# An FNet and Hyena encoder layer: another start of the Fourier stage, and the first batch's gate products on VectorE

## The chip, the cores and the metric

The kernel runs on one core of a Trainium2 chip. The metric is the device time of one execution in microseconds (us). The core has TensorE (PE, with its weight loads as PEld), VectorE (DVE), ScalarE (ACT), GpSimd (POOL) and SyncE (SP), which only starts transfers here. SP, ACT and POOL each have a queue of transfers of their own.

## What is computed

There are two batches, the prompt (b = 0) and the sample (b = 1), of 1024 rows with 1024 channels, in fp32. Each goes through the same layer:

```python
xn = rmsnorm(x, g_pre)
fv, fg, hv, hg, mg = split(xn @ w_in)
# Fourier branch: 4 groups of 256 channels
fz = real(fft2(fv.reshape(B, L, 4, 256), over rows and channels of a group, ortho))
y_f = (fz * silu(fg)) @ w_fourier_out
# Hyena branch: width-3 convolution, then two long gated convolutions
v, x1, x2 = split(short_conv(hv, w_short))
z = v
for n, gate in enumerate((x1, x2)):
    z = gate * long_conv(z, filters[n], hyena_d[n])   # two-sided, by FFT
y_h = (z * silu(hg)) @ w_hyena_out
g_f, g_h = split(sigmoid(mg + b_merge))
out = (g_f * y_f + g_h * y_h) @ w_out
y = x + rmsnorm(out, g_post)
```

The filters come from a small network with sine activations (`hidden`, two layers) and exponential decays.

## The kernel before

All products are made of fp32 operands split into a rounded high part and a remainder: `split` rounds on ScalarE (L171 in before) and subtracts on VectorE or POOL (L181), and `mm3` makes three matmuls of the four parts. `mm` is L194, so nearly all matmuls have that line; they are told apart by their tile names. Engines run their instructions in order. The order is made when the program is built, by a scheduler with a timeline of its own. `issue_after(i)` is the means against it: whatever is traced inside the block stands behind instruction `i` on `i`'s engine. Tiles have a tag and a number of buffers; a tile waits until its buffer's last user has finished.

The stages, by time in the profile:

- The Fourier stage (0 to some 225 us, `phase_fourier`). `hidden(0)` makes the filter network's first layer. `norm` loads x in eight row tiles of 128, squares each with a sum (`ss`), makes the reciprocal roots in two groups of four (`rstd`, many tiny VectorE instructions) and scales the identity by them (`dg`). `xtile(b, k)` makes channel tile k of the normalized x, transposed: eight matmuls of a row tile with `dg` (`tpx`), a scaled copy (`xg`, two buffers), a store to DRAM (`d_x`), the even and odd folding about the middle row (`eo`), and its split (`eh`, `el`). Row 512 of the folding goes into `x5` by itself, in two tiny VectorE instructions for each tile. `weights` loads and folds the columns of the Fourier projection (`wfv`, `wer`, `wor`; split into `we`, `wo`), in two halves. The products `pfv` of `begun` are accumulated tile by tile as `xtile` goes on, for the first batch only; six PSUM tiles are open then, and the other two odd ones follow. `fourier_half` then applies the row transform (`stage`, table `seq`: tiles `pse`, `pso`, `sev`, `sst`, `pp`, `qp`) and the channel transform (`pP`, `pQ`), and stores `fz`. The halves run as (0,0), (0,1), (1,1), (1,0).
- The main stage (`phase_main`, to some 765 us). It rebuilds split x from `d_x` (`xl`, `xh`), makes the filters' spectra (`pft`, `pXf`) and spills input projections for later (`spill_gate`, `pin`). Its first tables of the filters (`hid`, `w3s`, `ex`) come at the end of the Fourier stage.
- The branches (to some 1740 us, `branches`). 32 steps of long convolutions, 16 for each batch: projection and short convolution (`conv`), forward transform (`pX`), product with the spectrum (`t`, `y`, `yl`), inverse (`pT`). In the second convolution of the first batch, the gate x2 is multiplied by silu(hg) in two halves of 128x512 (`close`), on POOL.
- The gates of the second batch (`pg`) and the output stage (`phase_out`; `pyf`, `pyh`, then `po`). In the latter `gated` loads a gate tile `g`, and `ahead` loads and splits the operands of the next projection.

## Time and profile before

| | |
|---|---|
| median of 3 runs | 2445.93 us (2445.39 to 2446.81) |
| the profiled execution | 2449.26 us |
| its span | 2447.1 us |
| TensorE busy | 2396.1 us (98%), 13196 matmuls |
| VectorE busy | 1893.8 us (77%) |
| ScalarE busy | 1096.8 us (45%) |
| POOL busy | 485.9 us (20%) |
| transfers | 429.36 MB, 175 GB/s on average |

Busy times are by engine over the span; the profile also gives them for any stretch of time. A matmul's end is modelled, so that a busy TensorE need not be at its peak; the number of matmuls in a stretch says more. In a row of the groups or the timeline `out<-in` are the tiles, and what stands in brackets or behind the bar is the idle time of the engine before the instruction and who ended it.

### The profile page before, as it was taken

What the parts mean: (1) busy time and instruction counts of PE and PEld (TensorE: products, weight loads), DVE (VectorE), ACT (ScalarE), POOL (GpSimd) and SP (SyncE); (2) the same over time, 40 slices, a digit from 0 to 9 for tenths busy, and PEclk for the clock granted to TensorE, in tenths of its full rate; (3) what the DMA queues carried; (4) which work ended last, traced back from release to release, by engine and by line L of the source; (5) the groups of instructions that cost most, each with busy time, mean ns of one, the idle gap of its engine ahead of it and who ended that gap; (6) DMA issues with size and microseconds to landing.
All of it is one profiled execution on the core that took longest, in us unless ns stands there. A gap on an engine that the chain in (4) does not pass through costs nothing.

```text
span 2447.1 us, 36853 instructions
## 1 busy us (share of the span) xinstructions
PE 2396.1 (98%) x13196; PEld 2082.3 (85%) x13196; DVE 1893.8 (77%) x3405; ACT 1096.8 (45%) x2063; POOL 485.9 (20%) x516
## 2 busy tenths in 40 slices
PE   6999999999999999999999999999999999999998
PEld 5988888888888888888888888888788888888886
DVE  7687888888748999999989999766555455665677
ACT  5545677767633433334223333333344444544343
POOL 1341222222143433331000000112200111122111
PEclk9999999999999999999999999999999999999999
DMA  7545655555555555445434444335454567776543
GB/s 273 170 141 191 224 175 173 167 175 167 173 194 177 172 177 173 165 165 192 146 128 134 141 141 138 121 121 184 154 174 159 198 210 255 245 250 213 169 164 129
DMA packets 225151, 429.36 MB, mean 175 GB/s; under 512 B 23542, under 2 KB 87255, under 8 KB 224456
## 3 DMA queue, kind: packets, MB, share of 16 engines
q1 hardware_dynamic: 198444, 333.34, 41.1%
q0 software_dynamic: 26336, 93.65, 10.9%
q8 instruction: 104, 1.70, 0.3%
q14 instruction: 79, 0.65, 0.1%
q10 hardware_dynamic: 188, 0.02, 0.0%
HBM read 290.60 MB, written 136.31 MB: 174 GB/s over the span
## 4 chain that ended last, share of the span: by engine, by line
PE 88%; DMA 5%; issue 3%; DVE 2%; ACT 1%; POOL 1%; SPq 0%; DVEq 0%; POOLq 0%; ACTq 0%
PE pin L194 41%; PE pT L194 7%; PE pg L194 7%; PE pX L194 7%; PE po L194 6%; PE pyh L194 5%; PE pyf L194 5%; PE pXf L194 3%; PE pfv L194 2%; DMA wr<-in_w_fo 1%; PE pft L194 1%; PE tph L792 1%; DMA wr<-in_w_ho 1%; PE tpx L194 1%; DMA wfv<-in_w_fv 1%
## 5 line engine op out<-in xcount | busy, mean ns | idle before, releaser
L194 PE MATMUL pin<-xh,wl 128*128 128x512 f32 x1472 | 577.2, 392 | 2.6 <-POOL wl L181 2.6
L194 PE MATMUL pin<-xl,wh 128*128 128x512 f32 x1472 | 575.6, 391 | 2.4 <-DVE xl L181 2.4
L194 PE MATMUL pin<-xh,wh 128*128 128x512 f32 x1472 | 576.5, 392 | 0.7 <-DMA wh<-d_w 0.7
L181 POOL TENSOR_TENSOR wl<-wr,wh 128x512 fp32r<-128x512 f32 x136 | 240.3, 1768 | 1144.0 <-ACT wh L171 1105.9
L194 PEld LDWEIGHTS pin<-xh,wl 128*128 128x128 f32 x1472 | 277.1, 188 | 54.9 <-POOL wl L181 4.1
L194 PEld LDWEIGHTS pin<-xl,wh 128*128 128x128 f32 x1472 | 277.1, 188 | 54.3 <-DVE xl L181 3.2
L194 PEld LDWEIGHTS pin<-xh,wh 128*128 128x128 f32 x1472 | 277.1, 188 | 52.1 <-DMA wh<-d_w 1.1
L171 ACT CAST wh<-wr 128x512 fp32r<-128x512 f32 x264 | 162.8, 619 | 346.0 <-PE pin L194 136.8
L194 PE MATMUL pT<-cinv,yh 128*128 128x256 f32 x1024 | 193.1, 283 | 0.0
L194 PEld LDWEIGHTS pT<-cinv,yh 128*128 128x128 f32 x1024 | 164.0, 190 | 9.0
L181 DVE TENSOR_TENSOR t<-pX,k 128x1024 f32<-128x1024 f32 x128 | 155.9, 1218 | 10.9 <-PE pX L194 9.3
L194 PE MATMUL pX<-bh,cfwd 128*128 128x256 f32 x768 | 159.6, 286 | 0.0
L181 DVE TENSOR_TENSOR wl<-wr,wh 128x512 fp32r<-128x512 f32 x128 | 87.2, 687 | 93.5 <-ACT wh L171 93.2
L194 PE MATMUL pyf<-sf,wh 128*128 128x512 f32 x512 | 158.0, 390 | 0.9 <-ACT wh L171 0.9
L194 PE MATMUL pyh<-sh,wh 128*128 128x512 f32 x512 | 157.3, 389 | 0.0
L171 ACT CAST bh<-b 128x512 fp32r<-128x512 f32 x144 | 89.0, 620 | 126.7 <-DVE b L181 84.5
L194 PE MATMUL pT<-cinv,yl 128*128 128x256 f32 x512 | 144.9, 283 | 0.0
L171 ACT CAST yh<-y 128x512 fp32r<-128x512 f32 x128 | 79.2, 619 | 114.1 <-DVE y L181 91.3
L194 PEld LDWEIGHTS pX<-bh,cfwd 128*128 128x128 f32 x768 | 126.3, 190 | 2.5
L194 PEld LDWEIGHTS pyf<-sf,wh 128*128 128x128 f32 x512 | 96.0, 188 | 21.3 <-ACT wh L171 1.6
L194 PEld LDWEIGHTS pyh<-sh,wh 128*128 128x128 f32 x512 | 96.1, 188 | 19.9
L194 PE MATMUL pX<-bl,cfwd 128*128 128x256 f32 x384 | 109.6, 285 | 0.0
(354 smaller groups left out, 5262.7 us busy)
## 6 DMA issues: line engine op xcount, KB each, us to landing
k<-d_k SPq DMA_DIRECT2D x128, 512.0 KB, 4.0
wr<-in_w_in SPq DMA_DIRECT2D x136, 256.0 KB, 3.1
d_g<-gt SPq DMA_DIRECT2D x124, 256.0 KB, 2.6
d_k<-kt SPq DMA_DIRECT2D x128, 128.0 KB, 2.1
d_k<-kt SPq DMA_DIRECT2D x64, 256.0 KB, 2.3
wr<-in_w_fo POOLq DMA_DIRECT2D x64, 256.0 KB, 4.0
g<-d_g SPq DMA_DIRECT2D x64, 256.0 KB, 4.2
wr<-in_w_ho POOLq DMA_DIRECT2D x64, 256.0 KB, 3.7
```

Source lines behind the costliest of these rows:

```text
L171: self.rounded = nc.scalar.copy(h, src)
L181: return e.tensor_tensor(out, a, b, op=op)
L194: return self.nc.tensor.matmul(out, lhsT, rhs, start=start, stop=stop, skip_group_check=shared)
L792: nc.tensor.transpose(tp[:, q * P:(q + 1) * P], eo[:, e, q], self.ident)
```

## The change

It has eight parts.

1. At the start, the eight row tiles of x are loaded from SP's and ScalarE's queues in turn and ahead of all squares. The last square is made by VectorE. The sines of `hidden` and its store come behind ScalarE's last square. The first half's weights stand behind the scaled identity, and then behind each tile's folding.
2. The tables `seq`, `alt`, `chan` and `chx`, and four small ones from SP's queue (`vec`, `th`, `wsh`, `bm`), are all started by POOL behind a copy from tile 4. The copy writes into `seq` so that the order holds.
3. Row 512 of each tile is copied into `r5` by ScalarE, and `x5` is split once per batch.
4. The two odd products that came later (`begun[1, 2]`, `begun[1, 3]`) are started at tile 7, with all earlier tiles. The second batch has four open products too, two of them from the first tile on and two from tile 7. `p5` uses another tag of PSUM.
5. The squares of the second batch stand behind marks in the first batch's second half (`self.odd`, and the casts of weight steps 1 and 5) instead of behind its last cast.
6. `hid` is rounded behind the last products of the half (1, 1).
7. The products of x2 with silu(hg) move from POOL to VectorE.
8. In the output stage an operand's load stands behind the last gate tile's load on SP's queue.

```diff
@@ -174,7 +174,7 @@
         self.left = self.sub(eng, l, src, h)
 
     def stt(self, eng, out, a, s, b, op0=MUL, op1=ADD):
-        self.nc.vector.scalar_tensor_tensor(out, a, s, b, op0=op0, op1=op1)
+        return self.nc.vector.scalar_tensor_tensor(out, a, s, b, op0=op0, op1=op1)
 
     def tt(self, eng, out, a, b, op):
         e = self.nc.gpsimd if eng == "pool" else self.nc.vector
@@ -268,7 +268,7 @@
             self.stt("dve", y, k, -c, y)
         pi = 3.1415925
         nc.vector.tensor_scalar(y, y, pi, -pi, op0=ALU.min, op1=ALU.max)
-        nc.scalar.activation(out, y, AF.Sin)
+        return lambda: nc.scalar.activation(out, y, AF.Sin)
 
     def hidden(self, layer, px, pf):
 
@@ -292,19 +292,25 @@
             w, z = w[64:128], z[64:128]
...
+        sins = []
         for n in range(2):
             p = self.psum("mm", 4, "phd")
             nc.tensor.matmul(p, w, z[:, 512 * n:512 * n + 512], start=True, stop=True)
-            self.sin_of(y[n], k[n], out[n], p, self.hfb[:, 2 * layer:2 * layer + 1],
-                        self.hfb[:, 2 * layer + 1:2 * layer + 2])
-        nc.sync.dma_start(self.d_h if layer else self.d_h1, h)
-
-
-    def norm(self, b, px, pf):
+            sins.append(self.sin_of(y[n], k[n], out[n], p, self.hfb[:, 2 * layer:2 * layer + 1],
+                                    self.hfb[:, 2 * layer + 1:2 * layer + 2]))
+
+        def end():
+            for f in sins:
+                f()
+            nc.sync.dma_start(self.d_h if layer else self.d_h1, h)
+        return end
...
+    def norm(self, b, px, pf, marks):
         ss = px.tile([P, 8], F32, tag="ss", name=f"ss{b}")
         self.rs = rs = px.tile([P, 8], F32, tag="rs", name=f"rs{b}")
         self.diag = dg = px.tile([P, 8, P], F32, tag="dg", name=f"dg{b}", bufs=1)
@@ -314,15 +320,23 @@
                 x = pf.tile([P, D], F32, tag=("fA", "fB", "ee0", "ee1", "oo0", "oo1")[m], name=f"x0_{m}", bufs=1)
             else:
                 x = px.tile([P, D], F32, tag="x", name=f"x{b}_{m}", bufs=3)
-            nc.sync.dma_start(x, a[f"x{b}"][m * P:(m + 1) * P, :])
             self.xs.append(x)
+            if b == 0:
+                (nc.scalar if m % 2 else nc.sync).dma_start(x, a[f"x{b}"][m * P:(m + 1) * P, :])
+        for m, x in enumerate(self.xs):
+            if b:
+                nc.sync.dma_start(x, a[f"x{b}"][m * P:(m + 1) * P, :])
             sq = px.tile([P, D], F32, tag="xg", name="sq", bufs=2)
-            nc.scalar.activation(sq, x, AF.Square, accum_out=ss[:, m:m + 1])
+            if b == 0 and m == 7:
+                nc.vector.scalar_tensor_tensor(sq, x, 1.0, x, op0=MUL, op1=MUL, accum_out=ss[:, m:m + 1])
+            else:
+                with tc.issue_after(marks[(0, 0, 0, 1, 1, 1, 2, 2)[m]].ins) if b else ExitStack():
+                    self.squared = nc.scalar.activation(sq, x, AF.Square, accum_out=ss[:, m:m + 1])
             if m % 4 == 3:
                 q = slice(m - 3, m + 1)
                 self.rstd(px, rs[:, q], ss[:, q], 4)
                 for j in range(m - 3, m + 1):
-                    nc.vector.tensor_scalar(dg[:, j], self.ident, rs[:, j:j + 1], None, op0=MUL)
+                    self.scaled = nc.vector.tensor_scalar(dg[:, j], self.ident, rs[:, j:j + 1], None, op0=MUL)
 
     def xtile(self, b, k, px, fo):
 
@@ -342,15 +356,18 @@
                 m = 4 * n + q
                 self.mm(tp[:, q * P:(q + 1) * P], xk(m), self.diag[:, m], True, True)
             nc.scalar.activation(xg[:, 512 * n:512 * n + 512], tp, AF.Copy, scale=self.gpre[:, k:k + 1])
+        self.xg = xg
         nc.sync.dma_start(self.d_x[b][k], xg[:, 0:L])
+        nc.scalar.copy(fo["r5"][:, k:k + 1], xg[:, 512:513])
+        if k == 7:
+            r5 = fo["r5"].unsqueeze(2).to_broadcast([P, 8, 2])
+            self.split(fo["x5"][:, :, b:b + 33:32], fo["x5"][:, :, 2 + b:35 + b:32], r5, "dve", "act")
         eo = px.tile([P, 2, 2, 256], F32, tag="eo", name="eo", bufs=2)
         fw = xg[:, 0:512].rearrange("p (a r) -> p r a", r=2)
         bw = xg[:, 1024:512:-1].rearrange("p (a r) -> p r a", r=2)
         self.add("dve", eo[:, 0], fw, bw)
-        self.sub("pool" if b else "dve", eo[:, 1], fw, bw)
+        self.folded = self.sub("pool" if b else "dve", eo[:, 1], fw, bw)
         self.split(fo["eh"][:, k], fo["el"][:, k], eo, "dve", "act")
-        x5 = fo["x5"][:, k]
-        self.split(x5[:, b:b + 33:32], x5[:, 2 + b:35 + b:32], xg[:, 512:513].to_broadcast([P, 2]), "dve", "dve")
 
 
     def open_weights(self, pw):
@@ -396,10 +413,12 @@
                     for k in range(8):
                         self.pfv(p, e, m, k, W, fo)
                 self.split(X_[0][:, m], X_[1][:, m], p[:, :n], "dve", "act")
+                if (e, m) == (1, 1):
+                    self.odd = self.rounded
                 if e == (b + half == 0):
 
                     if m == 0:
-                        p5 = self.psum("X", 2, "pfx")[0:36, :260]
+                        p5 = self.psum(*(("mm", 4) if b + half else ("X", 2)), "pfx")[0:36, :260]
                     for k in (2 * m, 2 * m + 1):
                         for i in range(2):
                             self.mm(p5, fo["x5"][:, k], WE[i][:, k], k + i == 0, k + i == 8)
@@ -470,7 +489,7 @@
                 Ps = pf.tile([P, 258], F32, tag="fPs", name="fPs", bufs=2)
                 Pm = pf.tile([P, 258], F32, tag="fPm", name="fPm", bufs=1)
                 nc.scalar.copy(Ps[:, :w], pP)
-                nc.scalar.activation(Pm[:, :w], pP, AF.Copy, scale=vec[:, 11:12])
+                scaled = nc.scalar.activation(Pm[:, :w], pP, AF.Copy, scale=vec[:, 11:12])
...
@@ -479,9 +498,11 @@
                 w = (258, 254)[n]
                 r = slice(0, w)
                 self.stt("dve", A[:, 1024 - t0:1024 - t0 - w:-1], pQ[:, r], vec[:, 11:12], Ps[:, r])
-                self.stt("dve", B[:, 1024 - t0:1024 - t0 - w:-1], pQ[:, r], vec[:, 12:13], Pm[:, r])
+                summed = self.stt("dve", B[:, 1024 - t0:1024 - t0 - w:-1], pQ[:, r], vec[:, 12:13], Pm[:, r])
             nc.gpsimd.dma_start(self.d_fz[b][2 * gg], A[:, 0:1024])
             nc.gpsimd.dma_start(self.d_fz[b][2 * gg + 1], B[:, 0:1024])
+        if (b, half) == (1, 1):
+            self.third = summed, scaled
 
     def phase_fourier(self):
         tc, nc, a = self.tc, self.nc, self.a
@@ -494,6 +515,7 @@
             pf = es.enter_context(tc.tile_pool(name="ff", bufs=1, reuse_waits="tile"))
             fo = {}
             fo["x5"] = pc.tile([P, 8, 36], F32R, name="x5")
+            fo["r5"] = pc.tile([P, 8], F32, name="r5")
...
@@ -510,38 +532,62 @@
                 fo["eh"] = pe.tile([P, 8, 2, 2, 256], F32R, tag="eh", name="eh")
                 fo["el"] = pe.tile([P, 8, 2, 2, 256], F32R, tag="el", name="el")
                 if b == 0:
-                    self.hidden(0, px, pf)
-                with tc.issue_after(behind.ins) if b else ExitStack():
-                    self.norm(b, px, pf)
+                    end = self.hidden(0, px, pf)
+                self.norm(b, px, pf, marks if b else None)
+                if b == 0:
+                    with tc.issue_after(self.squared.ins):
+                        end()
                 begun = {}
                 if b == 0:
                     W = self.open_weights(pw)
                     for e, m in [(0, 0), (0, 1), (0, 2), (0, 3), (1, 0), (1, 1)]:
                         begun[e, m] = self.psum("X", 2, "pfv1") if e else self.psum("mm", 4, "pfv0")
+                else:
+                    for m in range(2):
+                        begun[0, m] = self.psum("mm", 4, "pfv0")
                 for k in range(8):
                     if b == 0:
-                        self.weights(pw, W, 0, k, True)
+
+                        with tc.issue_after((self.folded if k else self.scaled).ins), tc.issue_after(self.squared.ins):
+                            self.weights(pw, W, 0, k, True)
                     self.xtile(b, k, px, fo)
+                    if (b, k) == (0, 4):
+
+                        gate = nc.gpsimd.tensor_copy(fo["seq"][:, 0, 0:1], self.xg[:, 0:1])
+                        with tc.issue_after(gate.ins):
+                            nc.gpsimd.dma_start(fo["seq"], a["c_seq"])
+                            nc.gpsimd.dma_start(fo["alt"], a["c_alt"])
+                            nc.gpsimd.dma_start(fo["chan"], a["c_chan"])
+                            nc.gpsimd.dma_start(fo["chx"].rearrange("p a b c -> p (a b c)"), a["c_chx"])
+                            for t, n in ((self.vec, "c_vec"), (self.th, "c_th"), (self.wsh, "w_short"), (self.bm, "b_merge")):
+                                nc.gpsimd.dma_start(t, a[n])
+                    if (b, k) == (0, 7):
+
+                        for m in (2, 3):
+                            begun[1, m] = self.psum("T", 2, "pfv1")
+                            for j in range(7):
+                                self.pfv(begun[1, m], 1, m, j, W, fo)
+                    if (b, k) == (1, 7):
+
+                        for m in (2, 3):
+                            begun[0, m] = self.psum("mm", 4, "pfv0")
+                            for j in range(7):
+                                self.pfv(begun[0, m], 0, m, j, W, fo)
                     for (e, m), p in begun.items():
                         self.pfv(p, e, m, k, W, fo)
                 for half in ((0, 1), (1, 0))[b]:
-                    if b + half == 0:
-                        nc.sync.dma_start(self.vec, a["c_vec"])
-                        for t in ("seq", "chan"):
-                            nc.gpsimd.tensor_copy(fo[t][:, 0, 0:1], self.rs[:, 7:8])
-                        nc.gpsimd.dma_start(fo["seq"], a["c_seq"])
-                        nc.gpsimd.dma_start(fo["alt"], a["c_alt"])
-                        nc.gpsimd.dma_start(fo["chan"], a["c_chan"])
-                        nc.gpsimd.dma_start(fo["chx"].rearrange("p a b c -> p (a b c)"), a["c_chx"])
-                    elif b + half != 2:
+                    if b + half not in (0, 2):
                         W = self.open_weights(pw)
                         for k in range(8):
                             self.weights(pw, W, half, k, False)
-                        behind = self.rounded
+                            if b == 0 and k in (1, 5):
+                                marks.append(self.rounded)
                     self.fourier_half(b, half, W, fo, px, pf, begun)
                     begun = {}
+                    if b + half == 0:
+                        marks = [self.odd]
                     if (b, half) == (1, 1):
-                        self.hidden(1, px, pf)
+                        self.hidden(1, px, pf)()
 
 
     def butterfly(self, ws, xp, xm):
@@ -876,8 +922,9 @@
             self.hid = ws.tile([P, L], F32R, tag="q", name="hid", bufs=2)
             hid = ws.tile([P, L], F32, tag="q", name="hidr", bufs=2)
             nc.sync.dma_start(hid, self.d_h)
-            nc.scalar.copy(self.hid, hid)
-            self.sub("dve", self.hid[64:128], hid[64:128], self.hid[64:128])
+            with tc.issue_after(self.third[0].ins), tc.issue_after(self.third[1].ins):
+                nc.scalar.copy(self.hid, hid)
+                self.sub("dve", self.hid[64:128], hid[64:128], self.hid[64:128])
             taps = self.filter_taps(0, 0, self.filter_rates(0, 0, ws), ws)
             self.load_x(0, range(4, 8))
             self.cfw0 = mf.tile([P, 4 * P], F32, name="cfw0")
@@ -885,8 +932,6 @@
             nc.sync.dma_start(self.cfw0, a["c_fw0"])
             nc.gpsimd.tensor_copy(self.cfwd[:, 0, 0:1], self.xl[4][:, 0:1])
             nc.gpsimd.dma_start(self.cfwd, a["c_fwd"])
-            for t, n in ((self.th, "c_th"), (self.wsh, "w_short"), (self.bm, "b_merge")):
-                nc.sync.dma_start(t, a[n])
             plain = [(5, c) for c in range(8)] + [(6, c) for c in range(8)] + [(4, c) for c in range(NH)]
             fill = sorted([((2 * c + 1) / len(plain), t) for c, t in enumerate(plain)]
                           + [((2 * c + 1) / max(NF, 1), (0, c)) for c in range(NF)])
@@ -949,7 +994,7 @@
                     if early:
                         with tc.issue_after(self.rounded.ins):
                             nc.scalar.activation(sg[q], sg[q], AF.Silu)
-                    self.mul("pool", X[i][:, s], X[i][:, s], sg[q])
+                    self.mul("dve", X[i][:, s], X[i][:, s], sg[q])
         B = front(0)
         gates(0)
         for i, (b, n, c) in enumerate(steps):
@@ -1116,7 +1161,7 @@
             pool = lambda n: es.enter_context(tc.tile_pool(name=n, bufs=1, reuse_waits="tile"))
             self.open_mm(es, "pso")
             bl, sp, oc, sc, op = pool("bl"), pool("sp"), pool("oc"), pool("sc"), pool("op")
-            self.nw = 0
+            self.nw, self.fetched = 0, None
 
             def operand(i, nm, k):
 
@@ -1160,7 +1205,8 @@
                     if dt:
                         S_[-1] = rounded(S_[-1])
                 if dt < 8:
-                    S_.append(operand(i, nm, dt))
+                    with tc.issue_after(self.fetched.ins) if self.fetched else ExitStack():
+                        S_.append(operand(i, nm, dt))
 
             def gated(i, dt, ps, sec, bias, out):
                 b, half = units[i]
```

2 lines of the change are left out of this document (1 added, 1 removed).

## The prediction

> **What bounds the kernel now.** I read the page's head first, then busy time by stretches of time, then what TensorE waited for, then the timeline and the chain of waits of the stretches with holes.
>
> ```profile
> span 2447.1 us, 36853 instructions
> PE 2396.1 (98%) x13196; PEld 2082.3 (85%) x13196; DVE 1893.8 (77%) x3405; ACT 1096.8 (45%) x2063; POOL 485.9 (20%) x516
> ```
> ```profile
> 20.00:40.00 20.00, 12.95 (x83) 12.49 (x84) 15.90 (x49) 10.23 (x22) 1.67 (x7) 0.97 0.79 266
> ...
> 60.00:80.00 20.00, 20.00 (x167) 19.54 (x166) 11.41 (x30) 8.22 (x24) 8.62 (x10) 1.00 0.25 77
> ...
> 120.00:140.00 20.00, 16.29 (x134) 15.29 (x134) 18.40 (x37) 13.33 (x23) 9.54 (x13) 1.00 0.81 277
> ...
> 780.00:1100.00 320.00, 320.00 (x1952) 286.08 (x1950) 310.45 (x482) 122.86 (x220) 118.59 (x112) 1.00 0.51 169
> ```
>
> The columns of the stretches are PE, PEld, DVE, ACT and POOL. TensorE is the bound: it is never idle in the first batch's convolutions (780 to 1100), and the Fourier stage runs at 20 us for 167 matmuls (0.12 us each) where nothing is missing. Holes lie in the Fourier stage: 83 matmuls in the second 20 us, 134 at 120 to 140. VectorE has only 9.55 us of idle time in the 320 us of the convolutions, which matters for the last edit. TensorE's own waits say who makes the holes:
>
> ```profile
> PE tpx L194 <- DMA wfv<-in_w_fv: 9.8, 1, 9.8
> PE tpx L194 <- DVE dg L325: 5.1, 1, 5.1
> PE tpx L194 <- ACT xg L344: 3.5, 2, 2.6
> ...
> PE pse L194 <- DVE x5t L181: 2.5, 2, 2.1
> PE pP L194 <- issue: 2.3, 1, 2.3
> ```
>
> The first wait is put down to a weight load because that landed last; what the first matmuls of the transposes (`tpx`) really need is the scaled diagonal `dg`, and so the row norms.
>
> **The start.** In before, the last of eight squares on ScalarE begins at 18.98, because a table load and two sines (`hidden`) stand among the squares; the second four norms start at 20.15, their diagonals end at 24.77, and the first product `pfv` comes at 31.28.
>
> ```profile
> 1.23 4.72 SPq L317 DMA_DIRECT2D x<-in_x  x8
> ...
> 13.30 0.17 DVE L242 TENSOR_SCALAR rs_m<-ss 128x4 f32<-128x4 f32 x1 [0.21 <-ACT sq L320]
> 18.98 1.04 ACT L320 ACTIVATE sq<-x 128x1024 f32<-128x1024 f32 x1
> 20.15 0.17 DVE L242 TENSOR_SCALAR rs_m<-ss 128x4 f32<-128x4 f32 x1 [1.52 <-ACT sq L320]
> 23.89 0.88 DVE L325 TENSOR_SCALAR dg<-ident,rs 128x128 f32<-128x128 f32 x4
> 24.24 6.85 PE L194 MATMUL tpx<-dg,x 128*128 128x128 f32 x40 [5.09 <-DVE dg L325]
> 24.41 0.53 POOL L532 DMA_DIRECT2D seq<-in_c_seq  x1 [0.18 <-POOL chan L531]
> 25.15 0.41 ACT L171 CAST we<-wer 128x260 fp32r<-128x260 f32 x1 [3.24 <-DVE wer L181]
> 31.28 1.23 PE L194 MATMUL pfv<-we,eh 128*128 128x260 f32 x8 [0.18 <-ACT eh L171]
> ```
> ```profile
> 831.54 1.28 DVE L177 SCALAR_TENSOR_TENSOR x<-yc,invn,x 128x1024 f32<-128x1024 f32 x1
> ```
>
> In the changed order seven squares run in a row on ScalarE, the sines come behind them, and the eighth square is a VectorE instruction (1.28 us by the row of the same operation and size; before does not show it with an accumulated sum, and I take nothing more for that). VectorE's chain from the norms' first step to the end of the diagonals takes 24.77 - 20.15 = 4.6 us, with weight operations in between that now stand behind it. Alone it is eleven steps of 0.17 with some 0.04 between them (an estimate) and 0.88 for the diagonals: 3.2. So: first norms at 13.3 as now, 3.2 and one leftover step of the sine's argument (0.4) to 16.9, square 18.2, second chain to 21.4. That is 3.4 us before 24.77. Then ScalarE has two weight casts (k = 0) ahead of the second half of `xg` instead of eight: six casts of 0.41 are 2.5; I take 1.5, since they overlap and other members of that pipeline stay. First `pfv` 4.9 us earlier.
>
> The next hole is the 2.6 us that TensorE waits for `xg`. It comes from a store that lands at 37.64:
>
> ```profile
> 28.77 8.87 DMA d_x<-xg
> ...
> 69.95 0.37 ACT oo L171
> ```
> ```profile
> d_x<-xg SPq DMA_DIRECT2D x16, 512.0 KB, 3.7
> ```
>
> `xg` has two buffers, so the third tile waits until the first is stored; that store took 8.87 us where the median is 3.7, because the 2 MB table `seq`, issued at 24.41, and weights were in the DMA engines. The change starts these tables only behind tile 4, so the hole goes: 2.6. What is late next is the fifth step: on POOL eight table issues at 0.53 us (the `seq` row) stand ahead of tile 5's memset, 4.2 us of a step of 4.8 us ((69.95 - 31.28) / 8); I keep 1 us for it. Four of the eight are small tables that SP issued among the first weights before, and that no instruction needs for a long time. TensorE's idle time in these steps is filled by the two odd tiles' products, which ran after step 7 before, and VectorE loses the two-column `x5` operations of the first batch, of which the eight casts alone are 3.5 us (a row below); for both I take 2, about half of that. The x loads themselves: I count no gain for four of them going to ScalarE's queue, since SP has issued all eight by 5.95, while the fourth tile's square ends only at 13.3: transfers set the pace, not issuing. The cost, ScalarE issuing ahead of its first square, is covered by the same wait for data. The Trainium skill says the same against this edit (DMA: Bandwidth & Descriptors, "Issuing engines are not separate DMA queues": starting transfers from several engines saves the time to issue them alone); a reader who believed in doubled bandwidth would add some 3 us here, and I do not.
>
> Sum at the point where the first half's products are done (69.95 in before): 4.9 + 2.6 - 1 + 2 = **8.5 us**. Ends: 4 (the store's wait and the memset both stay) and 11.
>
> **Second batch's norms.** ScalarE stood 3.39 us for a row tile of x, with casts behind it that TensorE needs; the 2.3 us "issue" wait at `pP` follows from it.
>
> ```profile
> 90.35 1.06 ACT L320 ACTIVATE sq<-x 128x1024 f32<-128x1024 f32 x1 [3.39 <-DMA x<-in_x]
> ```
>
> The change puts squares 0 to 2 behind the odd products, 3 to 5 behind weight step 1, 6 and 7 behind step 5. Tiles 3 to 7 still wait for a free buffer, thus for the square three before. Behind a waiting square now stand the casts of weight steps 2 and 3, for which TensorE waits. I exchange one such wait for another: 0, between -2.3 and +3.4.
>
> **Second batch's tiles.** Here the small `x5` casts are on the chain itself, drawn out to 1.4 us:
>
> ```profile
> 124.14 1.41 DVE x L173
> ...
> 133.82 1.42 DVE x L173
> ...
> 140.56 1.43 DVE x L173
> ```
> ```profile
> L173 DVE CAST x<-xg 128x2 fp32r<-128x2 f32 x16 | 7.0, 440 | 0.0
> ...
> L320 ACT ACTIVATION_READ_ACCUMULATOR sq<-x 128x1 f32 x16 | 3.0, 189 | 0.0
> ```
>
> They become one-column copies on ScalarE and one split per batch. Three such steps are 4.3 us, and four products of the second batch's first half now fill TensorE between the transposes. ScalarE gets the copies (16 at 0.19 by its nearest one-column row, below) and is busy 13.33 of 20 us there. I take **3 us**; ends 0 and 4.5.
>
> **The handover to the main stage.** In before the filter's first tables run ahead of a cast that TensorE needs:
>
> ```profile
> 211.22 0.64 ACT hid L879
> ...
> 214.09 1.70 ACT ex L642 x4
> ...
> 216.08 0.43 DVE x5t L181
> ```
>
> That cost the 2.1 us of `pse` <- `x5t`. The new order has this cast first, but the same block of about 4.6 us now stands ahead of a later copy `sev`, with input projections to cover it. I take **1 us**; ends +1.5 and -2.1.
>
> **The products.** Sixteen products of 128x512 go from POOL to VectorE.
>
> ```profile
> 893.26 2.94 DVE L181 TENSOR_TENSOR b<-bs,xt 128x256 f32<-128x256 f32 x2
> 893.19 2.74 POOL L181 TENSOR_TENSOR x<-x,sg 128x512 f32<-128x512 f32 x2 [0.43 <-ACT sg L951]
> 836.47 0.75 DVE L181 TENSOR_TENSOR b<-bs,xt 128x256 f32<-128x256 f32 x2
> 836.27 3.80 POOL L181 TENSOR_TENSOR x<-x,sg 128x512 f32<-128x512 f32 x2 [0.16 <-ACT sg L951]
> L181 DVE TENSOR_TENSOR bs<-xt 128x512 f32<-128x512 f32 x12 | 8.2, 683 | 0.0
> ```
>
> At 0.683 they add 10.9 us to VectorE. But beside POOL's pair at 893.19 two VectorE operations took 2.94 instead of 0.75: 2.2 us of waiting that goes. At 836 POOL is the one that is drawn out, and VectorE loses nothing at that instruction. If half of eight pairs hold VectorE up, 8.8 come back and 2.1 remain, inside the 9.55 of idle time: **0**. The Trainium skill has this rule (GPSIMD Engine Reference, "Specifications": the SBUF interfaces are shared, with contention when the VectorE instruction has two SBUF inputs); the row at 893 has two and agrees. Had the engines nothing in common, all 10.9 would be new work, 1.4 beyond the idle time. That 1.4 is also my upper end; below 0 there is nothing to win, as TensorE has no idle time there.
>
> **The output stage.** Operand loads now queue behind the gate's load on SP.
>
> ```profile
> 2201.95 10.45 DMA g<-d_g
> ```
>
> A gate tile that took 10.45 us on the chain had them in front. I take **0.5 us**; ends 0 and 1.5.
>
> **Sum.** 8.5 + 0 + 3 + 1 + 0 + 0.5 = 13.0 us. The profiled execution took 2449.26 us, its span 2447.1 and 2.2 around it, 3.3 over the median of 2445.93. So 2436.3 in its terms, and **2432.9** as a median.
>
> **Rivals.** First, VectorE sets the pace of the Fourier stage, and an earlier TensorE only waits elsewhere. For it: 15.90 and 18.40 us busy in the two 20 us with holes. Against: 11.41 at 60 to 80, where TensorE is full. Then only VectorE's saved work counts, the 7.0 us of casts less what hides, and the time is about 2441.
>
> Second, the squares block ScalarE: each of tiles 3 to 7 waits 3.39 us with casts behind it, 17 us against the 2.3 of today. Then 14.7 is given back and the time is about 2447.6. Against: squares 0 to 2 now run before the weight casts of steps 2 to 7, so buffers come free and loads start earlier.
>
> Third, slower: the pair of products stands in VectorE's order until ScalarE has made its gate, with `y`, `t` and `yl` behind it, on which the inverse transforms wait. ScalarE itself waits for TensorE in this stage:
>
> ```profile
> 831.70 0.62 ACT L171 CAST wh<-wr 128x512 fp32r<-128x512 f32 x1 [2.90 <-PE pin L194]
> ```
>
> At 2.9 us and 1.37 for the pair, eight pairs make 34.2; less 9.55 idle it is 24.6, and 24.6 - 13.0 gives 2457.5. It decides from 8 x (1.37 + w) - 9.55 = 13.0, a wait w of 1.45 us per pair. Against: in the new order the pair follows a `yl` whose cast is just ahead of the gate on ScalarE.
>
> **How the numbers follow.** Forecast 0.77, first rival 0.10, second 0.06, third 0.07. About 0.2% (4.9 us) is what a measurement of this kernel can tell from no change, so faster means under 2441.0. All terms at their good ends give 8.4 us more (2.5 + 2.3 + 1.5 + 1.1 + 1.0), so 2424.5; all at their bad ends take back 15.3, so 2448.2, which needs six mishaps at once. The range is 2424 to 2442: it takes in the first rival and leaves out the other two and the last of the bad ends. Faster: the forecast (0.76 of 0.77) and half of the first rival, 0.81. Same: the other half, half of the second and the rest, 0.09. Slower: the third and the rest of the second, 0.10.
>
> **What would show it.** Right: the second norms start near 18.5, the first `pfv` near 26.4, no wait of 2.6 us for `xg`, the first half's products done near 61.5; no 1.4 us `x5` casts on the chain; the 780 to 1100 stage with the same TensorE rate and VectorE near 311 us. Wrong: `d_x` or a weight landing in 8 us at steps 5 and 6, ScalarE idle before a square of the second batch by over 3 us more than once, or matmuls waiting for `y` and `yl` in the convolutions.

## The result and the profile after

The changed kernel takes 2448.48 us (median of 22 runs, 2444.05 to 2451.49), the kernel before 2445.4 us in the same comparison (22 runs): a ratio of 1.0012, 95% interval 1.0006 to 1.0017, or 3.1 us slower. The forecast was 2432.9, with a range of 2424 to 2442. The two profiled executions differ the other way (2448.19 us after, 2449.26 before), because that of before was 3.9 us over its median. The page after, its head:

```profile
span 2446.1 us, 36798 instructions
...
PE 2398.3 (98%) x13196; PEld 2083.5 (85%) x13196; DVE 1893.3 (77%) x3393; ACT 1097.4 (45%) x2079; POOL 478.2 (20%) x503
```

Busy time by stretches of the changed kernel (columns PE, PEld, DVE, ACT, POOL, then TensorE's granted clock, the DMA share and GB/s):

```profile
20.00:40.00 20.00, 18.06 (x130) 17.86 (x131) 17.08 (x43) 13.73 (x29) 3.15 (x4) 1.00 0.59 210
40.00:60.00 20.00, 17.69 (x139) 17.50 (x138) 13.97 (x28) 10.76 (x21) 9.57 (x13) 0.91 0.87 302
52.00:54.00 2.00, 2.00 (x10) 2.00 (x11) 2.00 (x4) 1.78 (x3) 0.00 (x0) 0.50 1.02 420
60.00:80.00 20.00, 17.34 (x141) 16.44 (x140) 13.40 (x42) 12.69 (x33) 7.95 (x11) 1.00 0.74 240
260.00:280.00 20.00, 17.05 (x77) 13.56 (x76) 15.96 (x28) 8.29 (x16) 4.87 (x5) 1.00 0.79 275
780.00:1100.00 320.00, 320.00 (x1951) 285.88 (x1950) 310.52 (x492) 124.69 (x223) 106.59 (x100) 1.00 0.53 169
```

At 20 to 40 us there are 130 matmuls where before had 83: the start did come earlier. But 60 to 80, full before (167), has 141, and a new hole stands at 260 to 280. The convolutions (780 to 1100) are as they were. TensorE's waits from 0 to 300 us name the new holes:

```profile
PE pfv L194 <- ACT eh L171: 5.2, 4, 2.3
PE pfv L194 <- DVE we L181: 3.4, 3, 1.7
PE pin L194 <- ACT wh L171: 2.3, 1, 2.3
```

To compare kernels whose orders differ, I count TensorE's work from its records, each matmul with its usual pace (0.227 us for 512 columns, 0.119 for 256 to 260, 0.111 for a record of 128), and look when a kernel has begun so much work. The reference is the kernel with part 8 alone (below), which has the order of before up to the output stage. Its time is given, then how far each profile lies behind (+) or ahead (-), in us. Each column is one execution, and some lie off their kernel's median: part 8's 0.9 us over it, that of before 3.9 over, those of the gate by ScalarE and of the last column 1.4 under, and that of the late squares 2.1 under.

| work | part 8 | before | changed | gate by ScalarE | no open products | squares late | combined | gate, no open |
|---|---|---|---|---|---|---|---|---|
| 20 | 47.0 | +0.3 | -6.1 | -6.3 | -5.6 | -6.7 | -6.6 | -6.6 |
| 40 | 67.4 | +0.3 | -2.3 | -5.5 | -1.6 | -2.7 | -5.9 | -5.3 |
| 60 | 88.1 | +0.4 | +3.3 | +0.7 | +2.9 | -0.2 | -2.0 | -1.4 |
| 80 | 109.6 | +3.0 | +1.8 | -0.7 | +1.5 | -1.4 | -3.4 | -2.4 |
| 140 | 175.7 | +2.8 | +2.3 | -0.2 | -1.4 | -3.6 | -5.0 | -5.2 |
| 200 | 244.5 | +2.3 | +1.8 | -0.8 | -1.9 | -3.9 | +0.8 | -5.6 |
| 240 | 285.1 | +2.3 | +6.8 | +3.9 | -1.9 | +0.8 | +0.8 | -5.6 |
| 1000 | 1052.1 | +1.7 | +5.7 | +2.8 | -1.6 | -0.3 | +2.2 | -6.1 |
| 2000 | 2061.5 | +1.9 | +5.1 | +2.8 | +0.3 | -0.1 | +3.0 | -6.1 |
| 2300 | 2360.9 | +5.8 | +5.1 | +2.8 | +0.3 | -0.1 | +3.0 | -6.1 |

So the change wins 6 us in the first 41 us, has lost them and 3 more by 91, loses another 5 at the handover near 280, and nothing is lost in the 2000 us behind. The column of before shows that 3 us of its Fourier stage were that execution's own.

### The profile page after: what moved, and what is told of

It reads as the page before. It is cut to its first block, busy times and chain, and to the rows that moved or that the text cites. A ratio compares the mean times of both kernels' runs of the same rounds, so it can differ in the third digit from the quotient of the medians.

```text
span 2446.1 us, 36798 instructions
## 1 busy us (share of the span) xinstructions
PE 2398.3 (98%) x13196; PEld 2083.5 (85%) x13196; DVE 1893.3 (77%) x3393; ACT 1097.4 (45%) x2079; POOL 478.2 (20%) x503
## 4 chain that ended last, share of the span: by engine, by line
PE 52%; DMA 1%; DVE 0%; POOL 0%; issue 0%; ACT 0%; DVEq 0%; ACTq 0%; POOLq 0%
PE pin L194 16%; PE pg L194 7%; PE pyh L194 7%; PE pyf L194 7%; PE po L194 6%; PE pT L194 4%; PE pX L194 4%; PE tph L838 1%; DMA wr<-in_w_fo 0%; POOL wl L181 0%; DMA wh<-d_w 0%; DVE xl L181 0%; DVE o L177 0%; ACT s13h L171 0%; DVE rs_t L247 0%
## 5 line engine op out<-in xcount | busy, mean ns | idle before, releaser
L181 POOL TENSOR_TENSOR wl<-wr,wh 128x512 fp32r<-128x512 f32 x136 | 250.6, 1843 | 1185.4 <-ACT wh L171 1101.7
```

The lines of the kernel that those rows point to most:

```text
L181: return e.tensor_tensor(out, a, b, op=op)
```

## The experiments

Each difference is to the kernel before in the same comparison. The intervals are some 2.2 us to either side, and for a difference between two of these kernels some 3 us (an estimate from them). Smaller differences are not shown by the times; the table above then says where a profile won and lost, for one execution each.

| kernel | median | ratio to before, 95% | us |
|---|---|---|---|
| changed | 2448.48 | 1.0012 (1.0006 to 1.0017) | +3.1 |
| part 8 alone | 2442.49 | 0.9987 (0.9978 to 0.9996) | -3.1 |
| parts 7 and 8 alone | 2442.53 | 0.9991 (0.9982 to 1.0000) | -1.9 |
| parts 1 and 8 alone | 2445.30 | 1.0000 (0.9991 to 1.0008) | +0.9 |
| changed, gate by ScalarE | 2447.12 | 1.0006 (0.9997 to 1.0015) | +1.5 |
| changed, tables early | 2446.39 | 1.0004 (0.9996 to 1.0013) | +0.8 |
| changed, `cinv` late | 2449.18 | 1.0016 (1.0007 to 1.0025) | +3.6 |
| changed, no open products in batch 1 | 2442.82 | 0.9989 (0.9980 to 0.9998) | -1.6 |
| changed, squares late | 2444.79 | 0.9998 (0.9989 to 1.0007) | +0.4 |
| combined (gate, squares late, no open products) | 2445.88 | 1.0004 (0.9995 to 1.0013) | +0.5 |
| combined, tables early | 2447.00 | 1.0010 (1.0001 to 1.0019) | +1.6 |
| combined, taps behind | 2443.80 | 0.9994 (0.9985 to 1.0003) | -1.7 |
| gate by ScalarE, no open products | 2438.09 | 0.9970 (0.9959 to 0.9982) | -7.4 |

**The tables' gate.** In before a copy of this kind took 0.18 us:

```profile
23.92 0.18 POOL L531 CAST seq<-rs 128x1 fp32r<-128x1 f32 x1 [3.65 <-DVE rs L253]
```

In the changed kernel's timeline:

```profile
37.14 7.82 POOL L556 CAST seq<-xg 128x1 fp32r<-128x1 f32 x1 [0.62 <-ACT xg L358]
...
44.49 0.43 DVE L181 TENSOR_TENSOR wo<-wor,wo 128x256 fp32r<-128x256 f32 x1
...
48.57 0.60 POOL L563 DMA_DIRECT2D bm<-in_b_merge  x1
49.10 0.22 POOL L352 MEMSET xg<- 128x2 f32 x2
49.31 1.29 DVE L181 TENSOR_TENSOR eo<-xg 128x512 f32<-128x512 f32 x2 [4.39 <-POOL xg L352]
...
51.74 2.10 PE L194 MATMUL pfv<-we,eh 128*128 128x260 f32 x8 [2.31 <-ACT eh L171]
```

A copy of one element per partition holds POOL for 7.82 us and ends when VectorE has its first gap, at 44.92. Eight issues follow, then the memset for which VectorE waits 4.39 us; ScalarE's `eh` waits for VectorE, and TensorE waits 2.31 us for `eh`.

```diff
-                        gate = nc.gpsimd.tensor_copy(fo["seq"][:, 0, 0:1], self.xg[:, 0:1])
-                        with tc.issue_after(gate.ins):
-                            nc.gpsimd.dma_start(fo["seq"], a["c_seq"])
+                        nc.scalar.copy(fo["seq"][:, 0, 0:1], self.xg[:, 0:1])
+                        first = nc.gpsimd.dma_start(fo["seq"], a["c_seq"])
+                        with tc.issue_after(first.ins):
```


> The changed kernel, but the one-element copy from tile 4 into seq that opens the tables' issues is made by ScalarE instead of POOL; the other seven issues stand behind seq's. Theory A (in the changed kernel that copy held POOL for 7.82 us, 37.14 to 44.96, ending when VectorE went idle, and the issues and tile 5's memset behind it made the hole at 50): the issues start near 38, no wait of TensorE over 1 us for eh near 51, the granted clock near 50 to 55 is not 0.66, and the time is 3 to 4 us less than the changed kernel's 2448.5, near 2445. Rival B (the eight issues of 0.53 us themselves and the 2.8 MB of tables beside the weights make the hole, whoever opens them): the hole of some 2.5 us stays or moves to another tile, and the time is within 1 us of 2448.5.

2447.12. The hole at 51 is gone, and the table has 3.2 us more left at 40 than the changed kernel: theory A's mechanism holds. In time only 1.4 is left of the 3 to 4, which is inside the intervals. The eight issues still stand ahead of a memset here, and between 20 and 40 us of work this kernel loses 0.8 us, where the changed one loses 3.8: the copy made the loss, not the issues.

```diff
-                    if (b, k) == (0, 4):
...
+                    if b + half == 0:
+                        nc.sync.dma_start(self.vec, a["c_vec"])
+                        for t in ("seq", "chan"):
+                            nc.gpsimd.tensor_copy(fo[t][:, 0, 0:1], self.rs[:, 7:8])
```


> The changed kernel without part 2: seq, alt, chan and chx are started by POOL behind the copies from the norms, and vec, th, wsh and bm by SP, as in the kernel before. Theory A (part 2 costs more than it wins: its hole at 50 and late weights of the second half at 78 and 87 are some 6 us, what it removes is the 2.6 us wait for xg): the wait for xg of 2 to 3 us near 35 comes back, the holes at 50, 78 and 87 go, and the time is 2444 to 2446. Rival B (part 2 was worth its 2.6 us, and the loss is elsewhere, at the handover near 280): 2449 to 2451.

2446.39, 0.4 over the range of A and far from B, though the gain of some 2 us is inside the intervals. The hole at 51 is gone. A hole of 1.6 us stands near 35, but it is not the wait for `xg` that A named: TensorE waits for `el`, in front of which VectorE waited 1.42 us for a weight `wfv`.

```diff
+        nc.gpsimd.tensor_copy(fo["pc"][b][:, k:k + 1], xg[:, 0:1])
```


> The kernel before with part 8 and with one POOL copy of one element per partition added for each channel tile (16 in all, into tiles of their own), to see how long such a copy takes beside VectorE. Theory A (a POOL instruction that reads SBUF is held up as long as VectorE goes on without a gap with instructions of two SBUF inputs): copies of 0.18 us where VectorE is idle or has one SBUF input, and of several us, up to 8, in the first batch's tiles where VectorE folds and splits without a gap; the long ones end where VectorE has a gap. Rival B (the 7.2 to 8.1 us of the copy into seq are that copy's own: its rounding, its place in a 2 MB tile, or transfers into seq): all 16 copies under 0.5 us.

One run, 2443.3. Thirteen of the 16 copies took 0.18 to 0.65 us, three took more than a microsecond, among them these (with VectorE's casts):

```profile
48.05 1.56 POOL L346 CAST pc<-xg 128x1 fp32r<-128x1 f32 x1
...
49.48 0.16 DVE L173 CAST x<-xg 128x2 fp32r<-128x2 f32 x1
...
135.47 2.73 POOL L346 COPY pc<-xg 128x1 f32<-128x1 f32 x1 [2.30 <-ACT xg L344]
...
138.08 0.18 DVE L173 CAST x<-xg 128x2 fp32r<-128x2 f32 x1
```

B falls: copies into other tiles, rounded or not, are held up too. A holds in part. None reached 8 us. This order still has the tiny `x5` casts on VectorE, and the copies of 1.56 and 2.73 end with such a cast (49.61 and 49.64, 138.20 and 138.26). Part 3 moved them to ScalarE. That their removal is why the gate waited for 7.82 us is argued from these rows, not shown by a run: another small copy of VectorE, at 136.28, had not let POOL in, and the third long copy (1.14 us) ended at 52.09 beside a 128x2 instruction with two inputs (51.97 to 52.11).

**The start alone.**

```diff
-                        self.weights(pw, W, 0, k, True)
+                        with tc.issue_after((self.folded if k else self.scaled).ins), tc.issue_after(self.squared.ins):
+                            self.weights(pw, W, 0, k, True)
```

The diff shows part 1's last piece; its others are in it as in the changed kernel.

> The kernel before with parts 1 and 8 alone: the new order of loads, squares, sines and weights at the start, and the output stage's edit, which alone gave 2442.5. Theory A (the start's gain is real and lasts where nothing else is moved): the first product pfv near 28 to 29 instead of 31.3, and 2 to 4 us less in all, 2438.5 to 2440.5. Rival B (an earlier first half is given back within the second half, since VectorE and ScalarE are as full as TensorE there): the first product early, and the time within 1 us of 2442.5.

2445.30, 2.8 over part 8 alone in nominal time and 4.0 in the differences: worse than either theory, and clear of the intervals. Its lead was 3.7 us at 20 us of work; at 40 it was 1.7 us behind:

```profile
57.71 1.22 PE L194 MATMUL pfv<-we,eh 128*128 128x260 f32 x8 [1.45 <-ACT eh L171]
...
59.38 0.43 DVE L181 TENSOR_TENSOR wer<-wfv 128x260 f32<-128x260 f32 x1 [1.60 <-DMA wfv<-in_w_fv]
...
59.73 1.66 DVE L181 TENSOR_TENSOR el<-eo,eh 128x1024 fp32r<-128x1024 f32 x1
61.44 1.23 PE L194 MATMUL pfv<-we,el 128*128 128x260 f32 x4 [2.04 <-DVE el L181]
```

The second half's `wer` waits in VectorE's order for a load, ahead of the last tile's `el`, and TensorE waits for that.

**The squares.**

```diff
-                with tc.issue_after(marks[(0, 0, 0, 1, 1, 1, 2, 2)[m]].ins) if b else ExitStack():
+                with tc.issue_after(marks[0].ins) if b else ExitStack():
...
+                        marks = [self.rounded]
```


> The changed kernel without part 5: the second batch's squares stand behind the last weight cast of the first batch, as in the kernel before. Theory A (the squares at 65 to 82 stand ahead of casts of the second half's weights, and their norms ahead of VectorE's splits, and make the waits for we at 78, 82 and 87, about 4 us): these waits go, a wait of 1.3 to 2.5 us near 92 comes in their place, and the time is 1.5 to 3 us less than 2448.5. Rival B (the waits for we come from the late weights behind the tables): the waits at 78 and 87 stay, another is added near 92, and the time is 2448.5 to 2451.

2444.79, 3.7 less in nominal time and 2.7 in the differences, which is A's range, about as wide as the intervals. At 60 us of work it is 3.5 us ahead of the changed kernel, some of it perhaps this execution's own; the waits at 78 and 87 are gone, one of 1.6 stays at 81. But in the combined kernel late squares cost time (below): what they cost depends on what stands around them.

**The handover.** The changed kernel's timeline:

```profile
264.04 0.57 POOL L950 DMA_DIRECT2D cinv<-in_c_inv  x1 [0.80 <-DMA d_fz<-fB]
...
264.42 0.38 SPq L788 DMA_DIRECT2D wr<-in_w_in  x1
...
265.16 0.62 ACT L171 CAST wh<-wr 128x512 fp32r<-128x512 f32 x1 [0.90 <-issue]
...
277.85 0.62 ACT L171 CAST wh<-wr 128x512 fp32r<-128x512 f32 x1 [5.80 <-DMA wr<-in_w_in]
...
278.52 0.50 PE L194 MATMUL pin<-xh,wh 128*128 128x512 f32 x1 [2.33 <-ACT wh L171]
```

The weight `wr` that this cast needs was issued at 264.42, right behind the 3 MB of `cinv`, and lands at 277.75, when `cinv` has landed (277.56). From the cast of one weight to that of the next ScalarE goes 12.7 us (265.16 to 277.85), and TensorE's products do not last that long.

```diff
-                if i == min(2, nf - 1):
+                if i == min(8, nf - 1):
                     self.cinv = mi.tile([P, 2, INVW], F32R, name="cinv")
-                    nc.gpsimd.dma_start(self.cinv, a["c_inv"])
+                    with tc.issue_after(self.left.ins):
+                        nc.gpsimd.dma_start(self.cinv, a["c_inv"])
```


> The changed kernel, but the 3 MB table cinv is started some 25 weight steps later in the main stage. Theory A (the new handover puts cinv's 13.5 us of transfers in front of an input weight wr, which lands after 8 us, so that TensorE waits 2.3 us for wh and 0.6 for wl near 278 and loses 4.9 us between 250 and 300, against 0.7 in the kernel before): the wait near 278 goes, the later start of cinv costs under 1 us where it falls then, and the time is 4 us less than 2448.5, near 2444.5. Rival B (SP's order alone, the weight's load behind two filter loads that wait for VectorE, makes the wait): the wait near 278 stays, and the time is within 1 us of 2448.5.

2449.18: no gain, as B has it in time, but not for B's reason, since the wait that B keeps is gone. Between 220 and 300 us of work this kernel loses 0.1 us to part 8's, where the changed one loses 4.1. It gave 3.7 us back at 579:

```profile
573.56 8.55 POOL L181 TENSOR_TENSOR wl<-wr,wh 128x512 fp32r<-128x512 f32 x2 [7.72 <-ACT wh L171]
...
579.43 0.50 PE L194 MATMUL pin<-xh,wl 128*128 128x512 f32 x1 [1.77 <-POOL wl L181]
```

This is POOL held up beside VectorE again: two `wl` in 8.55 us, where one takes 1.28 alone. Behind it TensorE's granted clock was 0.50 from 581 to 583.

```diff
-                else:
-                    for m in range(2):
-                        begun[0, m] = self.psum("mm", 4, "pfv0")
...
-                    if (b, k) == (1, 7):
...
-                        p5 = self.psum(*(("mm", 4) if b + half else ("X", 2)), "pfx")[0:36, :260]
+                        p5 = self.psum("X", 2, "pfx")[0:36, :260]
```


> The changed kernel without the second half of part 4: the second batch has no open products, and p5 has its former tag. Theory A (these products move the whole order behind them, so that at the handover SP starts two input weights in a row behind two filter loads and two stores, and TensorE waits 2.3 us for wh near 278; in this kernel's order SP's loads of wr stand one by one again): no wait over 1 us for wh between 250 and 300, the second batch's tiles lose at most 2 us, and the time is 2444 to 2446, against 2448.5. Rival B (the open products fill the holes between the second batch's transposes, 2 to 3 us, and the wait near 278 is cinv's in any order): 2449 to 2452, with the wait near 278 still there.

2442.82, 4.7 less than the changed kernel, clear of the intervals and better than A. In the second batch's tiles it wins 2.9 us (from +1.5 at 80 us of work to -1.4 at 140), where the changed kernel loses 0.5, and at the handover it loses nothing; 260 to 280 is full:

```profile
260.00:280.00 20.00, 20.00 (x106) 17.16 (x105) 17.35 (x36) 8.79 (x19) 4.57 (x4) 1.00 0.83 312
```

`cinv` is still in front here: it starts at 263.74, and the weight issued at 265.62 lands with it, at 275.89. But the last cast of a weight was at 266.95, 9.0 us before the next at 275.97, and TensorE had products for so long. All profiles of the two kinds agree: the wait for `wh` is 2.0 to 2.3 us, with 12.4 to 12.7 us between the two casts, in the four kernels that have the second batch's open products and `cinv` in its place, and it is absent, with 8.9 to 10.6 us, in before, in part 8's kernel and in the five without these products. So in the built order the open products decide where `cinv` falls among the weights, and the wait follows from that.

**Products and output.** Both start from before.

```diff
-                    self.mul("pool", X[i][:, s], X[i][:, s], sg[q])
+                    self.mul("dve", X[i][:, s], X[i][:, s], sg[q])
```


> The kernel before with parts 7 and 8 alone: the products of x2 with silu(hg) on VectorE, and the output stage's edit, which alone gave 2442.5. Theory A (the products cost and win nothing, as forecast): within 1 us of 2442.5, no TensorE wait over 0.3 us between 780 and 1100, VectorE near 311 us busy there. Rival B (with POOL free of them the weight splits wl come earlier at the change of batch near 1136, where the changed kernel missed 1.2 us less than before): the hole of 1.95 us near 1135 goes or halves, and the time is 1 to 2 us less than 2442.5.

2442.53 against 2442.49: A. VectorE is busy 310.53 us in the stage. The hole near 1135 went, as B has it (one of 1.1 us stands at 1152), without a gain in the median.

```diff
-                    S_.append(operand(i, nm, dt))
+                    with tc.issue_after(self.fetched.ins) if self.fetched else ExitStack():
+                        S_.append(operand(i, nm, dt))
```


> The kernel before with part 8 alone: in the output stage an operand's load stands behind the last gate tile's load. Theory A (the profile of the changed kernel has 0.45 us of missing TensorE time between 2100 and 2250, that of before 4.25, so that part 8 won 3.8 us and the rest of the change lost about 7): near 2441.6, and no wait of over 0.5 us for a gate tile. Rival B (the 4.25 us were one execution's, as that run was 3.8 us over its median): within 1 us of 2445.4.

2442.49, theory A. Who waited for the gate tiles from 2170 to 2230, in before (first fence) and in the changed kernel:

```profile
  DMA g<-d_g: 12.6, 6
...
  ACT g L1170: 12.3, 5
  ACT wh L171: 3.1, 1
```
```profile
  DMA g<-d_g: 4.9, 4
...
  ACT g L1216: 4.9, 4
```

A waiting `g` on ScalarE held a cast `wh` 3.1 us in before. TensorE's own waits there are 1.2 us for a `wl` and 0.9 for a `wh`, and none in the changed kernel. The table agrees: before loses 3.9 us from 2000 to 2300 us of work, every kernel with part 8 none.

**The losses together.** The combined kernel has the three edits shown.

> The changed kernel with three of its losses undone at once: the one-element copy that opens the tables by ScalarE, the squares of the second batch behind the last weight cast as before, no open products for the second batch. Theory A (the three losses are separate and add: 1.6, 2.7 and 4.7 us less in the single runs, against +3.1 of the whole change): some 6 us under the kernel before, near 2439, faster than part 8 alone. Rival B (they are one loss, seen three times: whatever moves the order at the handover or at 50 gets the same 3 to 5 us): no better than 1 us under the best of the single runs, 2441.5 to 2443.

2445.88: both theories fall. By the medians it is worse than two of its parts, though not clear of the intervals. Its lead of 5 us lasts to 140 and is lost from 160 to 180:

```profile
205.16 1.01 PE L194 MATMUL pQ<-qp,chan 128*128 128x256 f32 x3 [3.75 <-DVE fB L177]
...
205.76 1.28 ACT L676 ACT_TABLE_LOAD   x1
207.06 1.70 ACT L676 ACTIVATE ex<-dec,vec 128x256 f32<-128x256 f32 x4
208.67 0.45 ACT L492 ACTIVATE fPm<-pP,vec 128x256 f32<-128x256 f32 x1
...
209.17 3.68 PE L194 MATMUL pfx<-we,x 128*36 128x260 f32 x16 [2.37 <-ACT fPm L492]
```

Over these two waits TensorE's granted clock was 0.50, from 205 to 215. With part 8 alone the wait for `fB` was 2.05 us. Why it is longer here, no run shows.

> As the combined kernel, but with the tables started as in the kernel before instead of behind tile 4 (part 2 undone). Theory A (gating the tables was worth the 2 to 3 us wait for xg near 35 once POOL's copy is out of the way): 1 to 2.5 us slower than the combined kernel, with that wait back. Rival B (the tables' 2.8 MB cost the same wherever they fall in the first 60 us): within 1 us of the combined kernel.

The edit is the one shown for early tables. 2447.00, 1.1 over the combined kernel: as A has it, though inside the interval. The hole near 35 is 1.7 us, again before `el` and not before `xg`.

```diff
                 self.sub("dve", self.hid[64:128], hid[64:128], self.hid[64:128])
-            taps = self.filter_taps(0, 0, self.filter_rates(0, 0, ws), ws)
+                taps = self.filter_taps(0, 0, self.filter_rates(0, 0, ws), ws)
```


> The combined kernel (2445.9), with the first filter's rates and taps too behind the last fPm and fB of the half (1,1), as part 6 has it for hid alone. Theory A (in the combined kernel the lead of some 4 us at 193 is lost at the handover because the table load and the exponentials ex, 205.76 to 208.67 on ScalarE, stand ahead of the last fPm, for which TensorE waits 2.4 us, and the clock is lower after it): that wait goes and the time is 2 to 4 us less, 2442 to 2444. Rival B (the handover is held by its transfers, the store of fB and the loads of the main stage, and another wait takes the place of this one): within 1 us of 2445.9.

2443.80, 2.1 less: the lower end of A, inside the intervals. The wait for `fPm` is gone, the 3.6 us for `fB` stays.

> The changed kernel with two of its losses undone: ScalarE makes the copy that opens the tables, and the second batch has no open products. Theory A (the order behind the first 60 us is the same as in the kernel without open products, 2442.8, so that the 1.5 to 3 us won at 50 stay): 2440 to 2441.5. Rival B (what is won before 190 is lost at the handover whatever the order): 2442.5 to 2444.

The edits are those of the two runs named. 2438.09: 7.4 us under before, beyond A, and the fastest kernel of all. Its lead lasts through the handover (-5.2 at 140, -5.6 at 240). Two pieces undone take the changed kernel from 3.1 us over before to 7.4 under: these 10.5 us are clear of the intervals. The combined kernel is this one with late squares, and 7.8 us slower. So the handover has no fixed toll: in the two cases read above, a weight behind `cinv` and the exponentials `ex` ahead of `fPm`, the place of single instructions in the built order decides what is left of a lead.

## Why the prediction was wrong

**The start (8.5).** The second norms begin at 19.25 (18.2 in the sum), their diagonals end at 22.3, 2.5 us earlier instead of 3.4; the first `pfv` comes at 29.09, not 26.4: 2.2 us are won, not 4.9. The step with 1.5 us for casts failed: nothing between diagonals and `pfv` had waited for them; in before ScalarE had done them when `xg` waited for TensorE (26.84). The `xg` wait went, as forecast, though the tables may not have been its only cause: with the tables early and the other parts in place it did not come back. In all 6.1 us are won at 20 us of work. The step that failed most is POOL's. "I keep 1 us" for eight issues ahead of a memset was about right: they took 4.3 us, and 0.8 us is lost where they stand without POOL's copy. The gate copy itself I had put at nothing; it had 0.18 us by its nearest row and took 7.82. With what follows (hole and clock) that is 3.8 us, from -6.1 to -2.3. I had also put the second half's weights at nothing. From 40 to 60 us of work every kernel with the new start but that of parts 1 and 8 loses 2.5 us or more, with late squares too; from 55 to 92 us VectorE waits 5.4 us for `wfv` in the changed kernel, and 0.8 with part 8 alone. No run separates that loss. The first rival, VectorE's pace, is not what was seen: at 60 to 80 VectorE is busy 13.40 us of 20.

**The squares (0, -2.3 to +3.4).** ScalarE waits 0.65 us for x in all, so what I feared, and the second rival, did not happen. Their work, eight times some 1.25 us between 65 and 82, stood ahead of weight casts: 2.7 us in its run, a cost inside the range, but not fixed, as the combined kernel shows.

**The second batch's tiles (3).** The drawn-out casts are gone, and without the open products 2.9 us are won there. The step that four open products "now fill TensorE between the transposes" failed in the changed order: with them 0.5 is lost. With the squares late it is otherwise: 2.2 are won with them (from -1.4 to -3.6), and 1.6 without (from -3.4 to -5.0).

**The handover (1, +1.5 to -2.1).** It lost 4 to 5 us, outside my ends. I priced the one block that I had seen in before and put the rest of the new order at nothing. What costs there is a weight that is issued right behind `cinv` and lands 13.3 us later, with TensorE's products used up 2.3 us before its cast is done.

**The products (0) and the output (0.5).** The first is right, with TensorE full and VectorE at 310.52 where 311 was forecast; the third rival's waits did not appear. The output was mis-sized: 3 to 4 us. I priced one gate tile, where a wait on ScalarE delays the cast behind it, and so TensorE.

**The base.** Rows like the 3.39 us wait for x were one execution's: part 8's profile, in the same order, has 1.58 as its longest. In it `pP` waits for no issue. The wait for `x5t` is not of that kind: it is 0.7 there, behind a stretch at half clock, but 2.1 again in the kernel with parts 1 and 8.

Without two of its pieces the change gives 7.4 us, where 13.0 was forecast for the whole. Of these 3.1 are part 8's, forecast at 0.5, so that some 4.3 are left for all else, forecast at 12.5. The two pieces cost 10.5 us, more than all the rest wins.

## What to carry to other kernels

A tiny instruction on a shared path is priced by what it may wait for, not by its length: look at what the neighbouring engine does without a gap, and at what is queued behind it. A lead in an early stage is worth only what the built order of the next stage leaves of it, so follow it through the trace in units of work done, and undo parts in pairs, since single losses need not add. Take the reference rows from more than one execution.

## What the runs showed of the hardware

POOL's hold-up beside VectorE has no fixed size: the one-element copy took 7.82, 7.70, 7.23 and 8.08 us in four kernels with VectorE's two-input work around it, and 0.18 in before, beside VectorE's `dg`, a TENSOR_SCALAR. The Trainium skill (SBUF — State Buffer, "Who interferes with whom") says that a VectorE instruction with two SBUF inputs contends with a GpSimd instruction that reads SBUF, and not with one that only writes. The rows agree: POOL's memsets just before and behind took 0.10 us (36.42 and 50.81), beside two-input instructions too. That one copy can wait while fifteen such instructions start one after the other, as in the changed kernel, is more than it says.

A hole can cost more than its length. After the 2.3 us wait at 51.7 TensorE's granted clock was 0.50 from 51.65 to 55.06, with 10 matmuls from 52 to 54 where before had 20, and it was 0.50 again from 281 to 283 behind the wait at 278. But the length alone does not decide it. The wait for `fB` at 208 to 211 was 2.03 us in before and 2.05 with part 8 alone, in the same order; behind it the granted clock was 1.00 in the one (211 to 214) and 0.50 in the other (208.74 to 212.15). A wait of 1.40 us at 77.5 in the combined kernel was followed by 0.50, one of 3.06 us at 122.9 in the combined kernel with early tables by 1.00. So a part of what one execution loses at a hole is that execution's own: half of 3.4 us, or some 1.7 us (an estimate from these stretches). The Trainium skill (TensorE: Matmul & The Clock Gate, "What's actually happening") gives one idle window of about 3.4 us as the condition for half clock; here shorter waits were enough in some executions, and waits of the same length were not in others.
